# A decoder layer's key projection as a pair of column groups, ahead of the attention projections

## The chip, the cores and the metric

The kernel runs on one core of a Trainium2 chip. The metric is the device time of one execution in microseconds (us), measured three times for the kernel before; lower is better. A profile of one further execution records every instruction with its start and duration, and every DMA packet.

## The reference

One decoder layer, 256 tokens of width 2048, all in float32:

```python
h = rms_norm(x, mix_norm_g)
z = h @ w_in
mq, mk, mv, mo, mi, mf, fq, fk, fv, ff = split(z)
ha = mlstm_chunkwise(mq, mk, mv, ig, lf)          # 4 heads of 256; gates ig, lf from mi, mf
ha = rms_norm(ha) * sigmoid(mo)
hb = forgetting_attention(norm(fq), norm(fk), fv, logf)   # 8 heads of 128; logf from ff
x = x + concat(ha, hb) @ w_out
x = x + (gelu(conv3(a)) * g) @ w_down             # a, g = split(rms_norm(x) @ w_up)
x = x + sigmoid(rms_norm(x) @ w_ple_gate) * (p @ w_ple_proj)
```

`w_in` has 7184 columns: mq, mk, mv, mo with 1024 each, then the gates mi and mf (8), fq, fk, fv (1024 each) and ff (8). Everything that this text is about happens in the product with `w_in` and in the two token mixers that eat its columns.

## The kernel before, in words

**Blocks.** Each large product is a list of blocks, run in order by `run_stream`. A block brings one piece of a weight matrix (128 x 1024 floats, 512 KB, or a bit less) from memory into a raw buffer, splits it into two parts, and feeds TensorE. The split keeps float32 accuracy on a fast matmul type: ScalarE (ACT) casts the piece to `hi` (L300), VectorE (DVE) subtracts to get `lo` (L302), and each product is three matmuls, left-hi by hi, left-hi by lo and left-lo by hi. There are three raw buffers (four more, `more`, while the attention columns are computed), four buffers of parts, and splits are written up to three blocks ahead of the block that is multiplied.

**Two kinds of groups.** A `token_group` computes 512 columns: 8 blocks, each two rows of 128 of the inner dimension, 12 matmuls of 512 columns a block (L356 to L358). A `pair_group` computes two neighbouring pieces of n columns at once: 12 plain blocks ("p") of 12 matmuls with n columns, and two *sevens* ("a" and "b", four blocks each), a Strassen-like scheme that does the work of 24 matmuls with 21, three products for each of seven, at the price of sums of weights on DVE (L440, L441, L451, L452) and of four extra PSUM banks P1, P5, P6, P7. When both sevens are done, `combined` turns these banks into four correction tiles `z_fox` in the tile `spare`, and when the whole group is done, `evac` and `added` bring result and correction together. The order of a pair group is written out as a string, `FOX_ORDER`: four p, then a and p in turn, then b and p in turn, and a last p. Sums of the left side, `S_h`, are made once and used by every pair group. The matmuls of both kinds of groups go through `three` (L367 to L369) or directly through `token_group`.

**Order of the stage.** First 512 columns from mi on (a token group, while x is loaded, normalised and turned); then three pair groups of 430, 430 and 428 columns, which finish the gates, fq, fk and fv (below: the fox groups); then token groups in pairs for mq, mk, mv and mo; then w_out as two pair groups of 512 columns.

**Side work.** The mixers themselves are generators in the deque `side`. After each block `pull(2)` runs two of their steps, taken in turn from the first two generators of the deque, also where a step only finds that it has to wait. `gate_math` computes the gates in seven steps and puts a row for each head into memory (`kept_rows`), from which `row` spreads it to all partitions; `fox_heads` runs the eight attention heads in two generators, six steps a head; `mlstm_scores`, `mlstm_out` and `mlstm_gate` run the mLSTM heads. Ahead of w_out's fifth block `pull_all` runs whatever is left. The framework under this plans each engine's order from its own model of when things are ready, so an engine's rows in the trace don't always stand in the order of the source.

**Turning tiles.** Heads need their queries and keys with features on partitions. `square` transposes 32 x 32 squares on DVE (L204), and `move` then sends 16 DMAs from the POOL (GpSimd) queue (L210) that put the squares in place. `qk_squares(pair)` does that for two attention heads (`qky` to `qkz`, in the tags "sq" and "col"), and its reader waits until seven blocks have passed (`since(7, ...)`). For mq, `qk_group` evacuates into `mz`, squares into `my` (both in `spare`) and moves straight into `mqT`; for mk it moves into a buffer of the tag "zb", and `mk_columns` copies that to `mkT` (L759).

Of the kernel before, what the change touches and what calls it, by code (L numbers as in the profile page):

```python
# [9 lines left out]
F32 = mybir.dt.float32  # L10
# [5 lines left out]
P = 128  # L16
# [15 lines left out]
FOX_ORDER = "pppp" "apapapap" "bpbpbpb" "p"  # L32
GATED = 1032

BLK = 1024
# [26 lines left out]
def layer_kernel(  # L62
# [133 lines left out]
    def squares(name):  # L196

        return mp.tile([P, NT, 4, 128], F32, tag="sq", name=name)
# [308 lines left out]
    with mixers:  # L507
# [72 lines left out]
        def fox_norm(name, off):  # L580
            def gen():
# [12 lines left out]
                for t in range(NT):  # L594
                    v = zz[:, t, off : off + 1024].rearrange("p (h d) -> p h d", h=FH)
                    dve.tensor_mul(v, v, r[:, t * FH : (t + 1) * FH].unsqueeze(2).broadcast_to([P, FH, FD]))
                    yield
            side.append(gen())

        qkz = {}  # L600

        def qk_squares(pair):

            y = squares("qky")
            for c, (zz, off) in enumerate(((z["fq"], 8), (z["fk"], 0))):
                for t in range(NT):
                    square(y, t, 2 * c, zz[:, t, off + pair * 256 : off + (pair + 1) * 256])
            qkz[pair] = gather(y, "qkz")

        g = {}  # L610

        def gate_math():
            def gen():
# [32 lines left out]
                for tt in range(NT):  # L646
                    pe.transpose(bk[:12, tt * P : (tt + 1) * P], aF[:, tt, :], ident)
                aFT = mp.tile([P, 512], F32, tag="qk", name="aFT", bufs=2)[:12, :S]
                dve.tensor_copy(aFT, bk[:12, :S])
                kept_rows("F", aFT)  # L650
                for h in range(2):
                    row("F", 4 + h)
                yield

                M = mp.tile([P, 512], F32, tag="qk", name="M", bufs=2)[:4, :S]
                dve.tensor_tensor_scan(out=M, data0=aFT[0:4, :], data1=aFT[0:4, :], initial=0.0,
# [8 lines left out]
                act.activation(em, m, AF.Exp, scale=-1.0)  # L665
                g.update(Fs=Fs, aF=aF, em=em)
                yield
            side.append(gen())

# [15 lines left out]
        def fox_heads():  # L685
            zv = z["fv"]

            def gen(heads):
                while "em" not in g:
                    yield  # L690
                scale = FD ** -0.5
                for h in heads:
# [7 lines left out]
                    taken.add(h)  # L700
                    if h ^ 1 in taken and h // 2 + 1 < FH // 2:
                        qk_squares(h // 2 + 1)
                    yield
# [41 lines left out]
                    yield  # L745
            qk_squares(0)
            side.append(gen(range(0, FH, 2)))
# [7 lines left out]

        def mk_columns(grp, start):
            while not since(7, start):
                yield
            act.copy(mkT[:, 4 * grp : 4 * grp + 4].rearrange("p k (a j) -> p k a j", j=32),  # L759
                     z["mk"][:, grp].rearrange("p a (k j) -> p k a j", j=32))  # L760
            mk_in.add(grp)
            yield

        def qk_group(name, grp):
            def f(t, b):
                act.activation(mz[:, t], b, AF.Copy, scale=r1["t"][:, t : t + 1])
                square(my, t, 0, mz[:, t])
                if t < NT - 1:
                    return
                if name == "mq":  # L770
                    move(my, mqT[:, grp])
                    return
                if grp == 0:
                    z["mk"] = zbuf("mk").rearrange("p t c -> p (t c)")[:, 0:2048].rearrange("p (g a c) -> p g a c", g=2, c=P)
                move(my, z["mk"][:, grp])
                side.append(mk_columns(grp, done[0]))
            return f
# [166 lines left out]

        z_fox = [spare[:, 2048 + 512 * i : 2560 + 512 * i] for i in range(4)]
        for g_, n in enumerate(FOX_HALVES):

# [19 lines left out]

            def combined(p1, p5, p6, p7, n=n):
                z_ = [v[:, :n] for v in z_fox]
                act.copy(z_[0], p1)  # L970
                dve.tensor_add(z_[1], p6, z_[0])
                dve.tensor_add(z_[2], p7, z_[1])
                for i in (1, 3):
                    dve.tensor_sub(z_[i], p5, z_[i // 2 + 1])

            blocks.extend(pair_group(w_in, lambda: hT, c0, n, FOX_ORDER, ("mm", "aux") if g_ % 2 == 0 else ("aux", "mm"),
                                     S_of, evac_half, added, combined))
            c0 += 2 * n
# [873 lines left out]
```

## Time and profile before

| | |
|---|---|
| median of 3 runs | 1228.82 us (1228.74 to 1228.92) |
| the profiled execution | 1229.07 us |
| its span, first to last instruction | 1227.4 us |
| TensorE (PE) busy | 1219.6 us, 99% |
| weight loads (PEld) busy | 1025.9 us, 84% |
| DVE / ACT / POOL busy | 1023.6 / 761.4 / 179.1 us |
| granted TensorE clock | 0.999 |
| DMA | 276.36 MB, mean 225 GB/s |

The span is the time between the core's first and last instruction; the execution's own time is 1.67 us longer. A matmul's row has the time from its start to the end that is modelled for it, and matmuls overlap: how fast PE works is read from the distance of their starts, not from the durations. The three fox groups run from 32.7 to 141.5 us of the span, mq to mo from there to 341.3 us, w_out to 432 us, and the feed-forward part and the last gate take the rest. Idle time of an engine is put down to what released it; a row of that kind for an engine that isn't the bottleneck costs nothing by itself.

### The profile page before, as it was taken

The page shows a single profiled execution, that of the slowest core. Times are in us where ns is not written, and L with a number is a line of the kernel's source. Part 1 is how long each engine was busy: PE and PEld are TensorE (multiplying, and loading weights), DVE is VectorE, ACT ScalarE, POOL GpSimd, SP SyncE. Part 2 cuts the span into 40 slices and gives each one's busy share as a digit, 9 for nine tenths or more (in the row PEclk, how much of TensorE's full clock was granted, in tenths as well). Part 3 has the DMA queues.
Part 4 walks back from the last instruction along what each step waited for, and adds up shares of the span by engine and source line. Part 5 has one row for each costly group of instructions (what it writes and reads, how often), then busy time and mean ns, then how long its engine had stood idle before and what let it go on. Part 6 is the DMA issues. An engine that isn't in the chain of part 4 may idle for free.

```text
span 1227.4 us, 16369 instructions
## 1 busy us (share of the span) xinstructions
PE 1219.6 (99%) x5547; PEld 1025.9 (84%) x5547; DVE 1023.6 (83%) x1287; ACT 761.4 (62%) x1115; POOL 179.1 (15%) x331
## 2 busy tenths in 40 slices
PE   9999999999999999999999999999999999999998
PEld 7999988888888888888888888888888888888887
DVE  6788857675679989788998898898788999999796
ACT  8567545565655665766676676757657555556653
POOL 2011237243301401011101101110110000050000
PEclk9999999999999999999999999999999999999999
DMA  9566677676565787777687678757796896876552
GB/s 307 181 197 195 175 229 222 183 218 194 164 234 179 234 254 238 241 220 239 202 274 240 188 252 265 229 174 223 236 315 238 293 374 205 268 248 209 193 206 68
DMA packets 126964, 276.36 MB, mean 225 GB/s; under 512 B 14793, under 2 KB 26817, under 8 KB 126881
## 3 DMA queue, kind: packets, MB, share of 16 engines
q1 hardware_dynamic: 115344, 257.27, 65.7%
q0 software_dynamic: 11008, 17.76, 5.2%
q8 instruction: 43, 0.70, 0.2%
q10 hardware_dynamic: 529, 0.30, 0.1%
q14 instruction: 40, 0.33, 0.1%
HBM read 247.99 MB, written 8.93 MB: 209 GB/s over the span
## 4 chain that ended last, share of the span: by engine, by line
PE 99%; DMA 0%; DVE 0%; SPq 0%; ACT 0%; issue 0%; DVEq 0%
PE up L369 12%; PE up L367 12%; PE up L368 12%; PE tg L357 6%; PE tg L356 6%; PE tg L358 6%; PE pg L367 5%; PE pg L368 5%; PE pg L369 5%; PE gt L369 2%; PE gt L368 2%; PE gt L367 2%; PE dnP L1349 1%; PE dnP L1350 1%; PE dnP L1348 1%; PE upP L369 1%
## 5 line engine op out<-in xcount | busy, mean ns | idle before, releaser
L368 PE MATMUL up<-part,x2T 128*128 128x512 f32 x608 | 236.6, 389 | 0.0
L369 PE MATMUL up<-part,x2T 128*128 128x512 f32 x608 | 236.1, 390 | 0.0
L1298 ACT CAST part<-raw 128x1024 fp32r<-128x1024 f32 (+1 forms) x144 | 145.3, 1020 | 104.7 <-PE up L369 36.3
L302 DVE TENSOR_TENSOR lo<-raw,hi 128x1024 fp32r<-128x1024 f32 (+3 forms) x119 | 139.2, 1173 | 76.9 <-ACT hi L300 76.6
L367 PE MATMUL up<-part,x2T 128*128 128x512 f32 x608 | 185.9, 389 | 0.0
L1300 DVE TENSOR_TENSOR part<-raw,part 128x1024 fp32r<-128x1024 f32 (+1 forms) x141 | 165.1, 1179 | 21.1 <-ACT part L1298 15.5
L300 ACT CAST hi<-raw 128x1024 fp32r<-128x1024 f32 (+3 forms) x119 | 120.2, 1012 | 97.4 <-PE tg L358 46.2
L368 PEld LDWEIGHTS up<-part,x2T 128*128 128x128 f32 x608 | 114.1, 188 | 23.7
L367 PEld LDWEIGHTS up<-part,x2T 128*128 128x128 f32 x608 | 114.1, 188 | 23.6
L369 PEld LDWEIGHTS up<-part,x2T 128*128 128x128 f32 x608 | 114.0, 188 | 23.5
L358 PE MATMUL tg<-hi,hT 128*128 128x512 f32 x288 | 113.6, 395 | 0.0
L357 PE MATMUL tg<-lo,hT 128*128 128x512 f32 x288 | 113.3, 393 | 0.0
L356 PE MATMUL tg<-hi,hT 128*128 128x512 f32 x288 | 112.4, 396 | 0.0
L210 POOL DMA_DIRECT2D EZ<-Y x66 | 35.2, 540 | 365.7 <-issue 204.7
L1298 ACT CAST part<-u36r 128x1024 fp32r<-128x1024 f32 (+1 forms) x46 | 47.9, 1044 | 34.6 <-PE up L369 17.2
L1300 DVE TENSOR_TENSOR part<-u36r,part 128x1024 fp32r<-128x1024 f32 (+1 forms) x46 | 55.6, 1209 | 9.4 <-ACT part L1298 5.2
L357 PEld LDWEIGHTS tg<-lo,hT 128*128 128x128 f32 x288 | 54.1, 188 | 11.1 <-DVE lo L302 0.2
L358 PEld LDWEIGHTS tg<-hi,hT 128*128 128x128 f32 x288 | 54.1, 188 | 10.9
L356 PEld LDWEIGHTS tg<-hi,hT 128*128 128x128 f32 x288 | 53.8, 188 | 10.7
L1300 DVE TENSOR_TENSOR part<-u32r,part 128x1024 fp32r<-128x1024 f32 (+1 forms) x44 | 50.3, 1148 | 14.1 <-ACT part L1298 11.6
L1298 ACT CAST part<-u32r 128x1024 fp32r<-128x1024 f32 (+1 forms) x44 | 43.3, 992 | 23.8 <-PE up L369 9.0
L368 PE MATMUL pg<-lo,hT 128*128 128x430 f32 (+1 forms) x156 | 55.7, 357 | 0.0
(924 smaller groups left out, 2770.7 us busy)
## 6 DMA issues: line engine op xcount, KB each, us to landing
raw<-in_w_up_dram SPq DMA_DIRECT2D x78, 512.0 KB, 4.9
raw<-in_w_in_dram SPq DMA_DIRECT2D x71, 512.0 KB, 4.3
u36r<-in_w_up_dram SPq DMA_DIRECT2D x43, 512.0 KB, 5.1
raw<-in_w_down_dram SPq DMA_DIRECT2D x41, 512.0 KB, 5.9
u32r<-in_w_up_dram SPq DMA_DIRECT2D x34, 512.0 KB, 4.9
xs<-in_w_up_dram SPq DMA_DIRECT2D x21, 512.0 KB, 4.9
w2b<-in_w_down_dram SPq DMA_DIRECT2D x20, 512.0 KB, 5.2
raw<-in_w_out_dram SPq DMA_DIRECT2D x17, 512.0 KB, 4.9
```

What stands on the lines that cost most here:

```text
L210: (other if other and (4 * a + b) % 3 else pool).dma_start(out=c[32 * b : 32 * b + 32, a::4], in_=y[32 * a : 32 * a + 32, :, b])
L300: act.copy(hi, raw)
L302: dve.tensor_sub(lo, raw, f32(hi))
L356: pe.matmul(o, ah, hi[:, i, :], start=first, stop=False)
L357: pe.matmul(o, ah, lo[:, i, :], start=False, stop=False)
L358: pe.matmul(o, al, hi[:, i, :], start=False, stop=last)
L367: pe.matmul(o, ah, hi, start=start, stop=False)
L368: pe.matmul(o, ah, lo, start=False, stop=False)
L369: pe.matmul(o, al, hi, start=False, stop=stop)
L1298: act.copy(r32(hi), raw)
L1300: dve.tensor_sub(r32(lo), raw, hi)
L1348: pe.matmul(o, ah, hi, start=first, stop=False)
```

## The change

mk, until now two token groups behind mq, becomes one pair group of twice 512 columns with two sevens, and it stands ahead of the three fox groups. It evacuates into the place of `mqT`, which is empty by then, takes its corrections from `z_fox`, squares into `spare` (the places of `mz` and `my`), and moves to the second half of `spare`, the place of `z_fox`. Its readers `mk_columns` wait for 9 and 12 blocks. The two PSUM tags of the fox groups change places. The queries and keys of the attention heads are squared in other places: pair 0 in `mqT`, as soon as fk is normalised; pair 2 in the second half of `spare`; pairs 1 and 3 as before; and each pair one pair earlier. `gate_math` is no longer in the deque: its seven steps hang behind mq's first five blocks, 2, 2, 1, 1 and 1 of them. The heads start when `Fs` is there, one step ahead of `em`. Two small tiles of the gates move to the tag "WT". `mlstm_scores` is appended behind mq.

```diff
+GATE_STEPS = (2, 2, 1, 1, 1)
...
+                if name == "fk":
+                    qk_squares(0)
...
-            y = squares("qky")
+            if pair % 2:
+                y, c_ = squares("qky"), mp.tile([P, NT * 4, 128], F32, tag="col", name="qkz")
+            else:
+                v = spare[:, 2048:4096] if pair else mqT.rearrange("p g a c -> p (g a c)")
+                y = v[:, 0:1024].rearrange("p (t b c) -> p t b c", t=NT, b=4)
+                c_ = v[:, 1024:2048].rearrange("p (a c) -> p a c", c=P)
...
-            qkz[pair] = gather(y, "qkz")
+            move(y, c_)
+            qkz[pair] = c_, done[0]
...
-                aFT = mp.tile([P, 512], F32, tag="qk", name="aFT", bufs=2)[:12, :S]
+                aFT = mp.tile([P, 384], F32, tag="WT", name="aFT", bufs=4)[:12, :S]
...
+                g.update(Fs=Fs, aF=aF)
                 yield
-                M = mp.tile([P, 512], F32, tag="qk", name="M", bufs=2)[:4, :S]
+                M = mp.tile([P, 384], F32, tag="WT", name="M", bufs=4)[:4, :S]
...
-            side.append(gen())
+            gate_steps.append(gen())
...
-                while "em" not in g:
+                while "Fs" not in g:
...
-                    if h ^ 1 in taken and h // 2 + 1 < FH // 2:
-                        qk_squares(h // 2 + 1)
+                    if h ^ 1 in taken and h // 2 + 2 < FH // 2:
+                        qk_squares(h // 2 + 2)
...
-            qk_squares(0)
+            qk_squares(1)
...
-        def mk_columns(grp, start):
-            while not since(7, start):
+        def mk_columns(grp, zk, start):
+            while not since(9 + 3 * grp, start):
                 yield
             act.copy(mkT[:, 4 * grp : 4 * grp + 4].rearrange("p k (a j) -> p k a j", j=32),
-                     z["mk"][:, grp].rearrange("p a (k j) -> p k a j", j=32))
+                     zk[:, grp].rearrange("p a (k j) -> p k a j", j=32))
...
+        def mk_group():
+            v = mqT.rearrange("p g a c -> p (g a c)").rearrange("p (t c) -> p t c", t=NT)
+            zk = spare[:, 2048:4096].rearrange("p (g a c) -> p g a c", g=2, c=P)
+            def evac(t, h, b):
+                act.activation(v[:, t, h * 512 : (h + 1) * 512], b, AF.Copy, scale=r1["t"][:, t : t + 1])
+            def added():
+                ys = [spare[:, i * BLK : (i + 1) * BLK].rearrange("p (t b c) -> p t b c", t=NT, b=4) for i in range(2)]
+                for h in range(2):
+                    for t in range(NT):
+                        w_ = v[:, t, h * 512 : (h + 1) * 512]
+                        dve.scalar_tensor_tensor(out=w_, in0=z_fox[2 * t + h], scalar=r1["t"][:, t : t + 1],
+                                                 in1=w_, op0=ALU.mult, op1=ALU.add)
+                for h in range(2):
+                    for t in range(NT):
+                        square(ys[h], t, 0, v[:, t, h * 512 : (h + 1) * 512])
+                for h in range(2):
+                    move(ys[h], zk[:, h])
+                    side.append(mk_columns(h, zk, done[0]))
+            return pair_group(w_in, lambda: hT, C_MK, 512, FOX_ORDER, ("mm", "aux"), S_of, evac, added, combined(512))
...
+        blocks.extend(mk_group())
         for g_, n in enumerate(FOX_HALVES):
...
-            blocks.extend(pair_group(w_in, lambda: hT, c0, n, FOX_ORDER, ("mm", "aux") if g_ % 2 == 0 else ("aux", "mm"),
-                                     S_of, evac_half, added, combined))
+            blocks.extend(pair_group(w_in, lambda: hT, c0, n, FOX_ORDER, ("aux", "mm") if g_ % 2 == 0 else ("mm", "aux"),
+                                     S_of, evac_half, added, combined(n)))
...
         for c in range(2):
-            add(C_MQ + c * 512, 512, qk_group("mq", c))
-        for c in range(2):
-            add(C_MK + c * 512, 512, after(qk_group("mk", c), *([mlstm_scores] if c else [])))
+            add(C_MQ + c * 512, 512, after(mq_group(c), *([mlstm_scores] if c else [])))
+        for i, n in enumerate(GATE_STEPS):
+            with_after(blocks[until + i], lambda n=n: [next(gate_steps[0]) for _ in range(n)])
```

More of the change, by code (lines that the diff above doesn't have):

```diff
@@ L607, in qk_squares @@
                     square(y, t, 2 * c, zz[:, t, off + pair * 256 : off + (pair + 1) * 256])
-            qkz[pair] = gather(y, "qkz")
+            move(y, c_)
+            qkz[pair] = c_, done[0]
         g = {}
+        gate_steps = []
         def gate_math():
@@ L665, in gen @@
                 act.activation(em, m, AF.Exp, scale=-1.0)
-                g.update(Fs=Fs, aF=aF, em=em)
+                g["em"] = em
                 yield
-            side.append(gen())
+            gate_steps.append(gen())
         kept, ready = {}, {}
@@ L754, in layer_kernel, with mq_group @@
         mk_in = set()
-        def mk_columns(grp, start):
-            while not since(7, start):
+        def mk_columns(grp, zk, start):
+            while not since(9 + 3 * grp, start):
                 yield
             act.copy(mkT[:, 4 * grp : 4 * grp + 4].rearrange("p k (a j) -> p k a j", j=32),
-                     z["mk"][:, grp].rearrange("p a (k j) -> p k a j", j=32))
+                     zk[:, grp].rearrange("p a (k j) -> p k a j", j=32))
             mk_in.add(grp)
             yield
-        def qk_group(name, grp):
+        def mk_group():
[17 more added lines that the diff above has]
+            return pair_group(w_in, lambda: hT, C_MK, 512, FOX_ORDER, ("mm", "aux"), S_of, evac, added, combined(512))
+        def mq_group(grp):
             def f(t, b):
@@ L767, in f @@
                 square(my, t, 0, mz[:, t])
-                if t < NT - 1:
-                    return
-                if name == "mq":
+                if t == NT - 1:
                     move(my, mqT[:, grp])
[L772 to L776, printed above, removed]
             return f
@@ L945, in layer_kernel, with combined, f @@
         z_fox = [spare[:, 2048 + 512 * i : 2560 + 512 * i] for i in range(4)]
+        def combined(n):
+            def f(p1, p5, p6, p7):
+                z_ = [v[:, :n] for v in z_fox]
+                act.copy(z_[0], p1)
+                dve.tensor_add(z_[1], p6, z_[0])
+                dve.tensor_add(z_[2], p7, z_[1])
+                for i in (1, 3):
+                    dve.tensor_sub(z_[i], p5, z_[i // 2 + 1])
+            return f
+        blocks.extend(mk_group())
         for g_, n in enumerate(FOX_HALVES):
@@ L966, in added @@
                     j()
[L968 to L974, printed above, removed]
-            blocks.extend(pair_group(w_in, lambda: hT, c0, n, FOX_ORDER, ("mm", "aux") if g_ % 2 == 0 else ("aux", "mm"),
-                                     S_of, evac_half, added, combined))
+            blocks.extend(pair_group(w_in, lambda: hT, c0, n, FOX_ORDER, ("aux", "mm") if g_ % 2 == 0 else ("mm", "aux"),
+                                     S_of, evac_half, added, combined(n)))
             c0 += 2 * n
```

## The prediction

> **What bounds the kernel now.** First the busy time by engine and the chain of work that ended last, from the page:
>
> ```profile
> PE 1219.6 (99%) x5547; PEld 1025.9 (84%) x5547; DVE 1023.6 (83%) x1287; ACT 761.4 (62%) x1115; POOL 179.1 (15%) x331
> ...
> PE 99%; DMA 0%; DVE 0%; SPq 0%; ACT 0%; issue 0%; DVEq 0%
> ```
>
> The chain is TensorE from one end to the other. The list of waits of TensorE over the whole span has two rows:
>
> ```profile
> PE xT L172 <- DMA xs<-in_x_dram: 1.5, 1, 1.5
> PE warm L110 <- DVE ones L106: 1.1, 1, 1.1
> ```
>
> Both lie in the first 10 us. The busy time of each stage (columns: stretch, its length, then busy us and count for PE, PEld, DVE, ACT, POOL, clock, DMA share, GB/s) says the same, with DVE at two thirds to four fifths:
>
> ```profile
> 32.70:141.50 108.80, 108.80 (x559) 104.87 (x558) 89.11 (x122) 71.13 (x143) 9.18 (x6) 1.00 0.60 181
> 141.50:341.30 199.80, 199.80 (x924) 166.52 (x923) 129.91 (x233) 110.37 (x182) 85.73 (x160) 1.00 0.72 206
> ...
> 1222.30:1227.40 5.10, 0.01 (x1) 0.00 (x0) 2.32 (x10) 0.70 (x2) 0.00 (x0) 0.86 0.26 85
> ```
>
> "Busy" could still hide slow matmuls, because their rows overlap. So I look at the distance of starts, in the timeline of PE around the seam from mo (a token group) to w_out (a pair group of 512 columns, the form that mk gets):
>
> ```profile
> 338.64 0.39 PE L356 MATMUL tg<-hi,hT 128*128 128x512 f32 x1
> ...
> 341.36 0.39 PE L367 MATMUL pg<-hi,catT 128*128 128x512 f32 x1
> ...
> 344.08 0.84 PE L367 MATMUL pg<-hi,catT 128*128 128x512 f32 x3
> ```
>
> Twelve matmuls lie between each two of these rows: 2.72 us for twelve, 0.2267 us each, in both forms. The time is therefore the number of matmuls times their step, plus 2.6 us at the start and 5.1 us at the end. An edit that lengthens other engines' work costs nothing until it makes TensorE wait, and none can gain more than the matmuls it removes or the waits that remain, and those lie before the change.
>
> **The change, part by part.** *mk as a pair group.* Two token groups are 16 blocks of 12 matmuls, 192. A pair group is 12 plain blocks of 12, 144, and two sevens of 21, 42: together 186. Six matmuls go, 6 x 0.2267 = **1.36 us**. The weights are the same 16 pieces of 512 KB, so the DMA load is the same, 192.5 GB/s at 2.72 us a piece.
>
> The Trainium skill, "TensorE: Matmul & The Clock Gate", section "Back-to-back issue gap", gives about 216 ns for 512 columns as the gap of matmuls alone and 131 ns for a sustained stream of loads and matmuls; by these the six would be 1.30 or 0.79 us. The trace has 227 ns, and the trace decides.
>
> *What the sevens cost elsewhere.* A seven splits 3.5 pieces for two and adds four sums of half a piece. Per pair of pieces that is 3.5 x 1.22 + 4 x 0.69 = 7.0 us on DVE against 21 x 0.2267 = 4.76 us on TensorE; with the plain block that stands between each two of its blocks (four of 1.22 us DVE, 2.72 us PE) the stretch has 11.9 us DVE in 15.6 us. The fox groups run at the same ratio, as all terms go with the number of columns, and let TensorE wait nowhere. So 0, hidden behind the plain blocks; the cover is gone if more than 3.7 us of other DVE work falls into one such stretch.
>
> ```profile
> L302 DVE TENSOR_TENSOR lo<-raw,hi x93: 1009/1224/1228, 29.6 to 343.2; 128x1024 fp32r<-128x1024 f32 x68, 128x860 fp32r<-128x860 f32 x17, 128x856 fp32r<-128x856 f32 x8
> L302 DVE TENSOR_TENSOR lo<-more,hi x35: 593/1049/1057, 32.1 to 136.2; 128x860 fp32r<-128x860 f32 x19, 128x856 fp32r<-128x856 f32 x10, 128x430 fp32r<-128x430 f32 x4, 128x428 fp32r<-128x428 f32 x2
> L1061 DVE TENSOR_TENSOR mqT<-pgP,mqT x2: 687/690/692, 381.5 to 416.4; 128x512 f32<-128x512 f32 x2
> L963 DVE SCALAR_TENSOR_TENSOR fv<-spare,rstd_mix,fv x6: 400/658/662, 108.3 to 146.3; 128x428 f32<-128x428 f32 x4, 128x176 f32<-128x176 f32 x2
> L204 DVE STREAM_TRANSPOSE spare<-spare x8: 670/705/711, 163.8 to 280.2; 128x512 f32<-128x512 f32 x8
> ```
>
> *The seam from mk to the first fox group.* Here DVE has `combined`, 4 x 0.69 = 2.8 us, and then `added`: four corrections, 0.66 x 512/428 = 0.79 us each, and four square transposes of 0.70, 6.0 us. TensorE then holds three split fox blocks of 12 x 0.195 = 2.34 us (step of the 430-column rows: 558 matmuls in 108.8 us), 7.0 us, and needs the fourth's `lo`, 1.05 us. If all of `added` stands before that split, 6.0 + 1.05 = 7.0: just in time. If `combined` is late as well, TensorE waits 2.8 us. Bounds 0 and 2.8; I take 0, because at the same seam of the first two fox groups the planner lets splits pass between the sums:
>
> ```profile
> 66.36 0.60 DVE L971 TENSOR_TENSOR spare<-pgP,spare 128x430 f32<-128x430 f32 x1 [0.72 <-PE pgP L369]
> 66.91 1.05 DVE L302 TENSOR_TENSOR lo<-raw,hi 128x860 fp32r<-128x860 f32 x1
> 67.89 0.60 DVE L972 TENSOR_TENSOR spare<-pgP,spare 128x430 f32<-128x430 f32 x1
> 68.40 1.05 DVE L302 TENSOR_TENSOR lo<-raw,hi 128x860 fp32r<-128x860 f32 x1
> ```
>
> *mk's move and `mkT`.* The same 32 DMAs from POOL and the same two copies on ACT of 1.05 us, but now inside the first fox group. POOL has room: it sat idle for 50 us before the norm of fq, its next work. What is new is the waiter: ACT's copies, behind which ACT's casts for the next blocks are queued.
>
> ```profile
> POOL r_fq L185 <- DVE rs_v L184: 50.2, 1, 50.2
> ...
> L210 POOL DMA_DIRECT2D mk<-spare x32: 536/536/558, 252.0 to 289.5; - x32
> L759 ACT COPY mkT<-mk x2: 1043/1052/1062, 279.0 to 299.3; 128x1024 f32<-128x1024 f32 x2
> ...
> 207.04 8.56 POOL L210 DMA_DIRECT2D qkz<-qky  x16 [4.20 <-ACT qk L698]
> ...
> 251.97 3.78 POOL L210 DMA_DIRECT2D mk<-spare  x7
> ...
> 265.32 0.54 POOL L210 DMA_DIRECT2D mk<-spare  x1 [2.65 <-issue]
> ```
>
> Counted from the seam, the squares of the first half are done at +3 to +5 us. Sixteen issues take 8.6 us (207.04) to 13.9 us (251.97 to 265.86), a landing 3.8 us. All 32 have landed at +24 to +37 us. In the source the second copy is due after the group's 11th block, +20.5 us (p 2.34, first block of a seven 0.59, the others 1.17). Bounds: 0 if the planner puts the copy in ACT's order behind the landing; if ACT is parked at it, the 15th block, due at +25.8, gets copy, cast and subtraction (1.05 + 0.85 + 1.05) after the landing: 1.2 to 14 us late. I take 0: in mk's stage before, the copies ran at 279.0 and 299.3, behind their moves (issued 252 to 266 and up to 290) and 30 to 40 us behind their turn in the source (after the 34th and 38th block of the stage, 3.1 us each: about 248 and 260), and neither that row nor any other ACT row between 33 and 341 us shows a wait for such a move. Deferred, the copy must still free the place of `z_fox` before the fox group's own `combined` at +33.4; at the high end it is 4 us late, and TensorE, which needs those banks for the next group at +36.3, waits up to about 2.4 us.
>
> *Gates and heads behind mq.* No matmul is added or removed: 8 heads, 4 mLSTM heads and the gates issue the same rows. Per run of small matmuls TensorE loses the same whether two heads' runs stand alone or together: here one head and two heads.
>
> ```profile
> 204.50 0.39 PE L357 MATMUL tg<-lo,hT 128*128 128x512 f32 x1
> ...
> 205.61 0.40 PE L356 MATMUL tg<-hi,hT 128*128 128x512 f32 x1
> ...
> 226.06 0.39 PE L356 MATMUL tg<-hi,hT 128*128 128x512 f32 x1
> ...
> 227.82 0.40 PE L358 MATMUL tg<-hi,hT 128*128 128x512 f32 x1
> ```
>
> Less two plain steps, one head's output costs 1.11 - 0.45 = 0.66 us, two together 1.76 - 0.45 = 1.31. So 0. The 48 blocks behind the fox groups (64 before) still hold the side work: gates fill the first blocks, 48 steps of the heads at two a block end at block 27, scores and outputs (16 steps and their waits) at block 37, and the mLSTM gates wait for mo as before; nothing more is left for `pull_all`. The same number of squares, moves and rows is issued. The mk groups' clash over `mz` and `my` goes, but TensorE did not wait for it.
>
> **Sum.** 1229.07 - 1.36 = 1227.71 us for the profiled execution (span 1227.4 - 1.36 = 1226.0); its median companion is 0.25 us lower: **1227.46 us**.
>
> **Rivals.** *A, slower: ACT parked at mk's copies.* Place: the first fox group, 20 to 35 us behind mk. It decides from a landing later than +22.9 us with the copy at its turn in the source. Price 1.2 to 14 us: 1228.7 to 1241.5 us, middle about 1235. For it: the landing is at +24 even at the fast rate. Against: the deferred copies above. [...] Chance 0.10.
>
> *B: the gain is spent at the seams.* DVE's 8.8 us behind mk, or the late place of `z_fox`, cost 1 to 2.8 us: 1228.5 to 1230.2 us. For it: just in time by my sum. Against: planned splits pass. Chance 0.10.
>
> *C, faster by more: TensorE's step falls.* The weight loads take 188 ns of each 227 and are busy 84%. If the blocks were paced by something that the new order removes, mk's 186 matmuls could run at 0.188: 1.36 + 186 x 0.039 = 8.6 us, 1220.2 us.
>
> ```profile
> L358 PEld LDWEIGHTS tg<-hi,hT 128*128 128x128 f32 x288 | 54.1, 188 | 10.9
> ```
>
> Against it: w_out's pair groups, the very form, step at 0.2267. The Trainium skill, "Perfetto Trace Analysis", section "Identifying the Most-Contended Engine", holds that matmul busy time misjudges TensorE and that the weight loads' share should be used; by it 16% would be open, but equal steps of 0.2267 in a stretch without waits say that the share is just 188 over 227. Chance 0.02.
>
> *D: crowded loads behind the fox groups.* With heads and gates earlier, more moves meet the loads while only three raw buffers are left. A load took 6.3 us there:
>
> ```profile
> raw<-in_w_in_dram SPq DMA_DIRECT2D x6, 512.0 KB, 6.3
> ```
>
> (median between 190 and 206 us, DMA 85% busy from 191 to 201). Three buffers give 8.16 us a round, less the split of 2.2 leaves 6.0; at 6.3 a block slips 0.1 us, covered by the three split blocks. At 10 us for a dozen blocks it would slip 16 us, 8 of them covered: 1235 us. Chance 0.03.
>
> **How the numbers follow.** Forecast 0.75, A 0.10, B 0.10, C 0.02, D 0.03. A measurement of this kernel tells about 0.2%, 2.46 us, from no change: below 1226.36 is faster, above 1231.28 slower. Faster: C and a little of the forecast's edge, 0.03. Slower: D, and the four fifths of A that cost over 3.8 us, 0.11. The rest, forecast and B included, is within: 0.86. The range takes the forecast's edge for unseen small terms on the low side (0.7 us) and B whole on the high one: 1226.7 to 1230.3; A's upper part, C and D are left out.
>
> **What would show it.** Right: PE steps of 0.227 in mk's rows (pair-group rows with 512 columns and hT from about 33 us), 186 of them in 42.2 us; no new row in TensorE's waits; span 1226.0. The seam: DVE rows L963 and L204 of mk with L302 among them. The copies L759 near 110 us without idle time ended by a DMA. A would show as idle ACT before L759 or a cast, followed by a PE wait for `lo`; B as a PE wait at the first or second fox group's start; D as casts waiting for raw. Wrong altogether: PE waits elsewhere, or steps that differ from 0.227.

## The result: 0.7% slower, and where the time went

The changed kernel takes **1237.18 us** (median of 6 runs, 1236.26 to 1239.11) against 1228.78 us (1228.62 to 1228.92) of the kernel before on the same chip: a ratio of **1.0069** with a 95% interval of 1.0059 to 1.0079. Predicted were 1227.46 us with a range of 1226.7 to 1230.3, and a chance of 0.11 for slower. The profiled execution took 1236.9 us, its span is 1235.2 us; the span before was 1227.4, so 7.8 us have to be found. Line numbers behind the change are some ten to thirty higher than before: L368 to L370 are the pair groups' matmuls, L357 to L359 the token groups', L301 and L303 the two halves of a split, L211 the moves, L222 and L223 the columns.

The page of the changed kernel, busy time and the chain of work that ended last:

```profile
PE 1224.1 (99%) x5541; PEld 1027.7 (83%) x5541; DVE 1036.7 (84%) x1307; ACT 765.4 (62%) x1122; POOL 177.7 (14%) x331
...
PE 94%; ACT 2%; DVE 2%; DMA 1%; issue 0%; ACTq 0%; DVEq 0%
```

The six matmuls are gone (5541 for 5547), yet PE is busy for 4.5 us more, and the chain, 99% PE before, now runs 5% through other engines. Both say that a stage has changed. Its list of PE's waits:

```profile
PE pg L368 <- ACT catT L222: 3.3, 1, 3.3
...
PE pg L368 <- DVE spare L980: 0.9, 1, 0.9
PE upP L368 <- DVE x2T L165: 0.7, 1, 0.7
```

These three rows are new. The starts of a few matmuls divide the span, here in the timeline of PE, the kernel before and then the one after; rows at the same place of the program:

```profile
141.44 0.35 PE L369 MATMUL pg<-hi,hT 128*128 128x428 f32 x1
...
427.05 0.39 PE L369 MATMUL pg<-hi,catT 128*128 128x512 f32 x1
...
1124.38 0.39 PE L367 MATMUL gt<-part,x3T 128*128 128x512 f32 x1
```

```profile
184.81 0.35 PE L370 MATMUL pg<-hi,hT 128*128 128x428 f32 x1
...
341.02 0.39 PE L368 MATMUL pg<-hi,catT 128*128 128x512 f32 x1
...
433.38 0.39 PE L370 MATMUL pg<-hi,catT 128*128 128x512 f32 x1
...
1132.20 0.39 PE L368 MATMUL gt<-part,x3T 128*128 128x512 f32 x1
```

With the first matmul of a token group (7.45 and 7.00 us) and the start of w_out before (341.36) the stages are:

| stage | before | after | difference |
|---|---|---|---|
| ahead of the first group | 7.45 | 7.00 | -0.45 |
| to the last matmul of the fox groups | 133.99 | 177.81 | +43.82 |
| to the first matmul of w_out | 199.92 | 156.21 | -43.71 |
| to the last matmul of w_out | 85.69 | 92.36 | **+6.67** |
| to the first matmul of the last gate | 697.33 | 698.82 | +1.49 |
| to the end | 103.02 | 103.00 | -0.02 |

The sum is +7.80. The move itself, 43.82 less 43.71, costs 0.11 us in place of gaining 1.36: a wait of 1.03 us at the second fox group, and 0.44 us that I did not trace. Two matmuls of `up` (0.45 us) stand ahead of w_out's last matmul before (383 PE rows in that stage) and behind it after (381), so w_out itself loses 7.1 us and the stage behind it 1.0. Nearly all is lost in w_out, in two ways. First the wait, in the timeline of PE after:

```profile
351.67 0.39 PE L370 MATMUL pg<-hi,catT 128*128 128x512 f32 x1
355.39 0.80 PE L368 MATMUL pg<-hi,catT 128*128 128x512 f32 x1 [3.33 <-ACT catT L222]
355.98 0.63 PE L369 MATMUL pg<-lo,catT 128*128 128x512 f32 x1
356.41 0.63 PE L368 MATMUL pg<-hi,catT 128*128 128x512 f32 x1
```

Between 351.67 and 355.39 lie 3.72 us where the step is 0.227: 3.49 us lost. Then the steps are 0.427 us: the rows follow each other at 355.98 and 356.41. That is the second way, and the windows show its reason in the granted clock (columns: stretch, length, busy us and count of PE, PEld, DVE, ACT, POOL, then the clock):

```profile
341.02:355.30 14.28, 11.04 (x49) 8.82 (x47) 8.72 (x16) 9.38 (x18) 6.28 (x12) 0.98 0.60 194
355.30:361.50 6.20, 6.11 (x18) 4.72 (x19) 6.20 (x13) 1.71 (x5) 0.00 (x0) 0.50 0.43 153
361.50:380.00 18.50, 18.50 (x83) 15.15 (x82) 15.54 (x21) 11.36 (x14) 0.00 (x0) 1.00 0.48 157
```

The clock stood at half from 354.7 to 361.5, 6.8 us. It fell 0.7 us before the wait ended, so 6.1 us of it lie on work, and about half of these, 3.0 us, is lost. That makes 6.5 of the 7.1 us; the rest is not traced.

What PE waited for are the columns 0 to 3 of `catT`, the first two mLSTM heads' output, which POOL moves and ACT casts. POOL and ACT after:

```profile
337.35 4.29 POOL L211 DMA_DIRECT2D haz<-hay  x8 [3.35 <-issue]
343.02 4.22 POOL L211 DMA_DIRECT2D haz<-hay  x8 [1.38 <-DMA haz<-hay]
347.26 1.43 POOL L186 TENSOR_TENSOR rh<-rs_v,neghalf 128x2 f32<-128x2 f32 x2
```

```profile
351.46 1.99 ACT L301 CAST hi<-raw 128x1024 fp32r<-128x1024 f32 x2 [2.66 <-DMA raw<-in_w_out_dram]
...
353.88 1.04 ACT L301 CAST hi<-morex 128x1024 fp32r<-128x1024 f32 x1
354.83 1.70 ACT L222 ACTIVATE catT<-haz,vT 128x256 fp32r<-128x256 f32 x4
```

The moves were issued from 337.4 to 347.2, around the start of w_out at 341.0. These moves took 3.2 to 5.4 us from issue to landing, 4.7 in the median, so the last can have landed by about 351.4; ACT, behind a load and four casts, reaches the columns only at 354.8, and PE wanted them at 351.9. So most of the 3.5 us is ACT's order: the columns stand behind the load's casts. The load itself is not new. In the kernel before, the same load ended ACT's wait 10.7 us behind the start of w_out, after the change 10.4, and PE lost nothing, because the columns stood ahead of it in ACT's order: the moves had gone out 8 us ahead of w_out, and the columns began at 343.1, nine microseconds before PE wanted them (four plain blocks behind 341.36, 10.9 us). Before:

```profile
L210 POOL DMA_DIRECT2D haz<-hay x16: 536/536/596, 323.2 to 332.8; - x16
L221 ACT ACTIVATE catT<-haz,vT x4: 499/502/512, 343.1 to 344.3; 128x256 fp32r<-128x256 f32 x4
```

```profile
352.01 2.01 ACT L300 CAST hi<-raw 128x1024 fp32r<-128x1024 f32 x2 [2.28 <-DMA raw<-in_w_out_dram]
```

The smaller wait, at the seam of the first and second fox group, after; timeline of ACT, PE and DVE:

```profile
115.32 1.03 ACT L771 COPY mkT<-spare 128x1024 f32<-128x1024 f32 x1
...
115.82 0.35 PE L370 MATMUL pg<-hi,hT 128*128 128x430 f32 x1
116.39 0.60 DVE L980 TENSOR_TENSOR spare<-pgP,spare 128x430 f32<-128x430 f32 x1 [1.49 <-ACT mkT L771]
...
117.05 0.46 PE L368 MATMUL pg<-hi,hT 128*128 128x430 f32 x1 [0.87 <-DVE spare L980]
```

The second copy of mk out of the place of `z_fox` runs at 115.3, though POOL had issued its last move by 101.1; DVE may write that place only behind it, and PE gets the banks 1.03 us late (1.23 less a step of 0.20).

### The profile page after: what moved, and what is told of

It is laid out like the page before. It is cut to its first block, busy times and chain, and to the rows that moved or that the text cites. A ratio compares the mean times of both kernels' runs of the same rounds, so it can differ in the third digit from the quotient of the medians.

```text
span 1235.2 us, 16364 instructions
## 1 busy us (share of the span) xinstructions
PE 1224.1 (99%) x5541; PEld 1027.7 (83%) x5541; DVE 1036.7 (84%) x1307; ACT 765.4 (62%) x1122; POOL 177.7 (14%) x331
## 4 chain that ended last, share of the span: by engine, by line
PE 94%; ACT 2%; DVE 2%; DMA 1%; issue 0%; ACTq 0%; DVEq 0%
PE up L370 11%; PE up L368 11%; PE up L369 11%; PE pg L368 5%; PE pg L369 5%; PE pg L370 5%; PE tg L357 4%; PE tg L358 4%; PE tg L359 4%; PE gt L370 2%; PE gt L368 2%; PE gt L369 2%; PE dnP L1382 1%; PE dnP L1381 1%; PE dnP L1380 1%; PE upP L368 1%
## 5 line engine op out<-in xcount | busy, mean ns | idle before, releaser
L370 PE MATMUL up<-part,x2T 128*128 128x512 f32 x608 | 235.6, 389 | 0.0
L303 DVE TENSOR_TENSOR lo<-raw,hi 128x1024 fp32r<-128x1024 f32 (+3 forms) x112 | 130.8, 1170 | 69.4 <-ACT hi L301 68.9
L368 PE MATMUL up<-part,x2T 128*128 128x512 f32 x608 | 185.4, 389 | 0.0
L301 ACT CAST hi<-raw 128x1024 fp32r<-128x1024 f32 (+3 forms) x112 | 112.6, 1008 | 91.8 <-PE pg L370 31.8
L368 PEld LDWEIGHTS up<-part,x2T 128*128 128x128 f32 x608 | 114.1, 188 | 23.6
L370 PEld LDWEIGHTS up<-part,x2T 128*128 128x128 f32 x608 | 114.0, 188 | 23.6
L358 PE MATMUL tg<-lo,hT 128*128 128x512 f32 x224 | 88.5, 395 | 0.0
L359 PE MATMUL tg<-hi,hT 128*128 128x512 f32 x224 | 87.9, 394 | 0.0
L211 POOL DMA_DIRECT2D EZ<-Y x66 | 35.2, 540 | 359.2 <-issue 205.1
L357 PE MATMUL tg<-hi,hT 128*128 128x512 f32 x224 | 86.6, 394 | 0.0
L369 PE MATMUL pg<-lo,hT 128*128 128x430 f32 (+2 forms) x208 | 76.0, 365 | 0.0
L370 PE MATMUL pg<-hi,hT 128*128 128x430 f32 (+2 forms) x208 | 75.7, 365 | 0.0
L1332 DVE TENSOR_TENSOR part<-u32r,part 128x1024 fp32r<-128x1024 f32 (+1 forms) x44 | 50.3, 1146 | 12.5 <-ACT part L1330 10.7
L368 PE MATMUL pg<-hi,hT 128*128 128x430 f32 (+2 forms) x208 | 58.5, 366 | 0.9 <-DVE spare L980 0.9
L303 DVE TENSOR_TENSOR lo<-more,hi 128x860 fp32r<-128x860 f32 (+5 forms) x46 | 45.5, 1007 | 14.8 <-ACT hi L301 14.7
```

What stands on the lines that cost most here:

```text
L211: (other if other and (4 * a + b) % 3 else pool).dma_start(out=c[32 * b : 32 * b + 32, a::4], in_=y[32 * a : 32 * a + 32, :, b])
L301: act.copy(hi, raw)
L303: dve.tensor_sub(lo, raw, f32(hi))
L357: pe.matmul(o, ah, hi[:, i, :], start=first, stop=False)
L358: pe.matmul(o, ah, lo[:, i, :], start=False, stop=False)
L359: pe.matmul(o, al, hi[:, i, :], start=False, stop=last)
```

## The experiments

The theory after the traces, the **late side chain**: gates, heads, scores and outputs form a chain that needs its time; mk's 16 blocks no longer stand between its start (the end of the fox groups) and its customer (w_out), so its end comes too late. Rivals: the **seam** (mk's place collides with the fox groups), and **crowding** (the gates in mq's blocks and the new moves hold the heads up). A third, late loads of w_out, is weakened by the load's rows above: it comes no later than before.

**pe_heads**: heads 0 and 1 go as heads 2 and 3 do, turned by PE.

```diff
-                early = heads[0] == 0
+                early = False
```

> The changed kernel, with the gated outputs of mLSTM heads 0 and 1 turned by TensorE (two runs of four 128x128 transposes, as heads 2 and 3 have it) in place of eight square transposes on DVE, 32 moves and four columns. Late side chain (the mk blocks that stood between the heads and w_out are gone, so those columns come late, TensorE waits 3.3 us for them and then runs at half clock): the wait for catT L222 goes, the granted clock stays at 1.00 through w_out, about 7 us come back less about 1 us for eight more transposes: 1230 to 1231.5 us. Seam theory (the cost is mk's late place at the second fox group, about 115 us): 1236.5 to 1238 us. Crowded gates and heads: they end as late as now and TensorE waits for the transposed heads instead, 1234 to 1238 us.

Measured 1231.66 us, 0.2 above the range, ratio 1.0023 (1.0013 to 1.0032); full clock through w_out. PE's waits and the 16 transposes of the four heads:

```profile
PE pg L368 <- DVE spare L980: 0.9, 1, 0.9
PE upP L368 <- DVE x2T L165: 0.6, 1, 0.6
```

```profile
L909 PE MATMUL hap<-ident,mv x16: 270/272/273, 342.3 to 348.6; 128*128 128x128 f32 x16
```

The wait and the half clock are gone, though ACT still waits 1.4 us for the same load (to 351.1). The w_out wait owns the loss. Without the moves, heads 2 and 3 are early too (at 348.6 done; 361.9 in the changed kernel): their `rh` no longer stands behind the moves in POOL's queue. What keeps this kernel 2.5 us of span behind the kernel before (the stages as above: +0.3, +43.5, -43.7, +1.1, +1.3) is the wait at the seam, the eight transposes more, which I put at 1 us by eight steps of the `hap` kind, and the last stage ahead of the gate, of which below.

**zk_mqT**: mk's squares go to the place of `mqT`.

```diff
-            zk = spare[:, 2048:4096].rearrange("p (g a c) -> p g a c", g=2, c=P)
+            zk = mqT
```

> The changed kernel, with mk's moved squares in mqT's place (2,048 elements, free from mk's squares to the first squares of q and k) in place of the upper half of spare, where the fox groups' z_fox stands. Late side chain: only the wait of about 1.0 us at the end of the first fox group goes, 1236.0 to 1236.4 us, the wait in w_out stays. Seam theory: if the delay there is what shifts all behind it, 1228 to 1230 us.

Measured 1237.05 us, 1.0071 (1.0056 to 1.0086): no difference from the changed kernel, and 0.65 us above the range, which had counted the wait at the seam as gained. The wait at the seam is gone, and the fox groups end 1.1 us sooner behind the first group. But w_out's wait has grown, with the half clock behind it:

```profile
PE hap L909 <- ACT catT L222: 5.9, 1, 5.9
```

What PE gains ahead of w_out the side chain doesn't gain: w_out starts sooner (2.3 us of that are ten of the mLSTM outputs' matmuls, `mob`, which now stand behind its start) and waits longer. The seam is not the cause.

**gates_deque**: the gates' steps as ordinary side work.

```diff
-            gate_steps.append(gen())
+            side.append(gen())
...
-        for i, n in enumerate(GATE_STEPS):
-            with_after(blocks[until + i], lambda n=n: [next(gate_steps[0]) for _ in range(n)])
```

> The changed kernel, with the gates' steps back in the queue of side work in place of mq's first five blocks (the heads still start at Fs, the new places of the squares stay). Late side chain: the cover is as short as in the changed kernel, and the gates come no earlier than before: 1236 to 1241 us, with the wait for catT L222 at least as long. Crowded gates and heads: without the hooks the chain runs as before, 1228 to 1231 us.

Measured 1245.63 us, 1.0140 (1.0124 to 1.0155), above the range given. PE's waits:

```profile
PE hap L909 <- DVE mv L906: 7.4, 1, 7.4
...
PE hap L909 <- ACT junk L877: 2.2, 1, 2.2
```

The hooks behind mq's blocks are worth 8.4 us here; crowding by the hooks is refuted. They don't quicken the gates themselves (the row of gates was turned 25.7 us behind the fox groups here, 25.8 in the changed kernel) but the heads: the last head's output came 151 us behind the fox groups, against 129. Why the heads gain so much is not shown.

**gates_only**: the kernel before with that part of the change alone (hooks, heads waiting for `Fs`, new places of the squares), mk as before.

> The kernel before, with the gates and heads of the change alone (gates' steps behind mq's first five blocks, heads start at Fs, first squares at fk's norm, even pairs of squares in their own places); mk stays two token groups behind mq. Late side chain: 64 blocks of cover stay, the columns are there long before w_out, 1228.3 to 1229.3 us, no new wait. Crowded gates and heads: slower by itself, 1231 us or more, with the heads' end or a wait of TensorE to show it.

Measured 1228.68 us, 1.0002 (0.9992 to 1.0011), no new wait. The gates' edit is free where 64 blocks follow, as the prediction had it.

**late_cols** and **late_cols_mqT**: w_out's first group takes the columns of heads 2 and 3 first, without and with the `zk` of above.

```diff
-OUT_K = (8, 9, 10, 11, 12, 13, 14, 15, 0, 1, 2, 3, 4, 5, 6, 7)
+OUT_K = (8, 9, 10, 11, 12, 13, 14, 15, 4, 5, 6, 7, 0, 1, 2, 3)
```

> The changed kernel, with w_out's first group taking catT's columns 4 to 7 (turned by TensorE) before columns 0 to 3 (the moved ones): the moved columns are wanted four plain blocks and half of the second seven later, some 15 us. Late side chain: the wait for catT L222 goes, and with it the half clock; what may be left is a shorter wait for heads 2 and 3 (hap), below 2 us and without half clock. 1229.5 to 1232 us. If w_out waits for something else that is late (raw loads, the sums S_o), the order changes nothing: 1236 to 1238 us.

> The changed kernel, with both: mk's moved squares in mqT's place, and catT's columns 4 to 7 ahead of 0 to 3 in w_out's first group. Late side chain: no wait at the second fox group (1.0 us less than late_cols) and none at half clock in w_out; what the six matmuls bring can show: 1227.5 to 1230 us, against 1228.7 of the kernel before. If the two halves of the loss are one cause, it is no better than late_cols alone: 1229.5 to 1232 us.

Measured 1240.19 us, 1.0092 (1.0076 to 1.0107), and 1238.11 us, 1.0071 (1.0059 to 1.0084). Both missed what the late side chain was given, and late_cols lies above even the 1236 to 1238 us of "something else that is late": not the moved columns alone are late. The wait of PE in late_cols (in late_cols_mqT `hap` waits 5.4 us), then its DVE:

```profile
PE hap L909 <- DVE mv L906: 6.5, 1, 6.5
```

```profile
351.93 1.23 DVE L303 TENSOR_TENSOR lo<-raw,hi 128x1024 fp32r<-128x1024 f32 x1 [1.82 <-ACT hi L301]
...
357.75 1.67 DVE L906 SCALAR_TENSOR_TENSOR mv<-mv,rh,mo 128x256 f32<-128x256 f32 x4
```

The gating of heads 2 and 3 (L906) stands on DVE behind the split and the weight sums of the second seven, and these behind the load that ACT waited for. So the load has a part in the wait, as the rival had it, though it comes no later than in the kernel before.

**hold_cols**: late_cols_mqT, with the moved columns held back in the side work until heads 2 and 3 are turned.

```diff
-                    side.append(columns(gather(y, "haz"), lambda: catT, 0, g_ml))
+                    side.append(behind(columns(gather(y, "haz"), lambda: catT, 0, g_ml)))
+                else:
+                    ha["turned"] = True
...
+        def behind(cols):
+            while "turned" not in ha:
+                yield
+            yield from cols
```

> The kernel late_cols_mqT, with the moved columns 0 to 3 held in the queue of side work until heads 2 and 3 are turned, so that on DVE their subtractions stand behind the gating of heads 2 and 3. Late side chain, and what the run late_cols showed (the order of w_out's blocks brings nothing while DVE's own order keeps heads 2 and 3 behind the late columns): hap runs near 350 us, the columns at 354 are wanted only at about 368, no wait above 1 us in w_out and full clock: 1228 to 1230 us. If the wait has another owner (sums S_o, raw loads of w_out): above 1233 us.

Measured 1238.03 us, 1.0076 (1.0063 to 1.0089), in the range of "another owner"; `hap` waits 6.3 us. The edit did not change what it aimed at: L906 stood ahead of the columns' subtractions on DVE already in late_cols (357.75 and 359.33), and does so here (356.18 and 357.76). POOL and DVE of this kernel:

```profile
347.90 2.11 POOL L211 DMA_DIRECT2D haz<-hay  x4 [0.25 <-DMA haz<-hay]
350.02 2.81 POOL L186 TENSOR_TENSOR rh<-rs_v,neghalf 128x2 f32<-128x2 f32 x2
```

```profile
355.57 0.69 DVE L477 TENSOR_TENSOR S_o<-So_f,S_o 128x512 fp32r<-128x512 f32 x1 [0.69 <-ACT S_o L476]
356.18 1.67 DVE L906 SCALAR_TENSOR_TENSOR mv<-mv,rh,mo 128x256 f32<-128x256 f32 x4
```

The norm of heads 2 and 3 (`rh`, L186) stands behind the 16 moves on POOL, and L906 then behind splits and sums on DVE, one of them waiting for `S_o`. These three edits of the customers' order helped nothing; that none could, because the tail of the chain is late on ACT, POOL and DVE at once, is my reading and not shown.

**mk_tokens_ahead**: mk at its new place, but as the two token groups of before, squares in `my`, moves into the same `zk`.

```diff
-        blocks.extend(mk_group())
+        for c in range(2):
+            add(C_MK + c * 512, 512, mk_tokens(c))
```

> The changed kernel, with mk at its new place ahead of the fox groups but as the two token groups of the kernel before (no sevens, six matmuls more). It tells the move from the form. Late side chain (the move costs, the form does not): w_out waits as in the changed kernel, and its half clock follows, while the wait at the second fox group may go, since mk's moves start earlier and half by half: 1235.5 to 1239 us. If the form (sevens, its burst on DVE) is what costs: 1228.5 to 1231 us.

Measured 1238.20 us, 1.0075 (1.0061 to 1.0088), with the wait in w_out and none at the seam:

```profile
PE hap L909 <- ACT catT L222: 6.5, 1, 6.5
```

So the **move** costs, not the form. One small thing goes with the form: from w_out's last matmul to the last gate this kernel takes 697.38 us, as before, and every kernel with the pair group 0.9 to 1.7 us more; in each of them PE waits for `x2T` at the first `up` groups (0.2 to 0.9 us). The two matmuls of `up` that stand inside w_out before and in this kernel, and behind it in the others, are 0.45 us of it; why `x2T` is late is open.

**cover**: the changed kernel with 196 matmuls more in mv's blocks, with a zero matrix on the left.

```diff
+                if bi and len(starts) == 8 and C_MV <= c0 < C_MO:
+                    for i in range(14):
+                        pe.matmul(st["b"][i % 2][:, :n], Zr, hi[:, 0, :], start=False, stop=False)
```

> The changed kernel, with 196 matmuls of a zero 128x128 against the block's own hi (512 columns) added to mv's two groups, 14 in each block behind the first of a group: 44.4 us of TensorE that load nothing and change nothing, in place of the 43.5 us that mk's blocks took out from between the heads and w_out. Cover theory (the side chain needs its time, whatever the blocks compute): the wait for catT L222 and the half clock go, 44.4 - 3.5 - 3.4 = 37.5 us, 1274 to 1276 us. If the chain is late for another reason (its order, its queues, DMA): the waits stay, 1280 to 1283 us.

Measured 1276.13 us. The 44.4 us of added work cost 38.95 us: 5.5 are given back (6.3 by the stages from w_out's start on). From the fox groups to w_out are 201.78 us now, and from w_out's start to the last gate 784.9 in place of 791.2, full clock. PE's waits, then the moves and ACT's columns:

```profile
PE upP L374 <- DVE x2T L165: 0.9, 1, 0.9
PE pg L374 <- DVE spare L986: 0.9, 1, 0.9
```

```profile
L211 POOL DMA_DIRECT2D haz<-hay x16: 533/534/596, 371.7 to 382.1; - x16
L222 ACT ACTIVATE catT<-haz,vT x4: 498/500/503, 389.3 to 390.5; 128x256 fp32r<-128x256 f32 x4
```

The moves go out 5 us ahead of w_out (387.5) again, and ACT's columns begin 1.7 us behind its start, as before the change. The added matmuls load nothing and feed nothing; they give back time, and the wait and the half clock vanish. By itself this would fit anything that lacks time ahead of w_out, the loads too; with the load's rows (no later than before) and pe_heads (no moves, no wait) it decides for the late side chain. The total is 0.1 us above the range, since the added rows took 45.57 us of the stage, not 44.4.

**pulls3**: three steps of side work behind each block for two.

```diff
-        run_stream(blocks, 2, more, ramp=True)
+        run_stream(blocks, 3, more, ramp=True)
```

> The changed kernel, with three steps of side work taken behind each block in place of two. It tests the count that the prediction used (steps per block) as what sets the end of heads and outputs. If steps per block set it, the heads end a third earlier in the order, the moves of haz go out well before w_out and the wait and the half clock go: 1229.5 to 1231.5 us. If the chain is set by its own latencies and its places in the queues (each head waits for moves, rows and the head before it), the heads end within some 10 us of where they do now and w_out still waits: 1234 to 1240 us.

Measured 1241.41 us, 1.0096 (1.0079 to 1.0113), 1.4 above the range of the second case; w_out waits 8.5 us, at `hap`. The matmuls of the heads' outputs, as groups with the first and last start, in the kernel before, the changed one and this one:

```profile
L741 PE MATMUL ob<-PT,fv x16: 377/378/382, 204.7 to 283.9; 128*128 128x256 f32 x16
```

```profile
L753 PE MATMUL ob<-PT,fv x16: 377/378/382, 260.0 to 314.1; 128*128 128x256 f32 x16
```

```profile
L753 PE MATMUL ob<-PT,fv x16: 377/378/382, 259.0 to 313.6; 128*128 128x256 f32 x16
```

Behind the end of the fox groups the last one comes at 142.5, 129.3 and 129.3 us. Half as many steps again per block change nothing: the steps that the source takes per block don't set the heads' end here. What does set it was not isolated.

**pe_heads_mqT**: both repairs at once.

> The kernel pe_heads, with mk's moved squares in mqT's place as in zk_mqT. Both losses gone at once. If they add up: pe_heads less 1.0 us, 1230.3 to 1231.0 us, no wait of TensorE but the one at the first up group (0.2 to 0.7 us). If removing the seam only moves the wait elsewhere, as it did in zk_mqT: 1231.5 us or more.

Measured 1231.71 us, 1.0020 (1.0010 to 1.0029), not told apart from pe_heads, and in the range given for a wait that moves elsewhere. The list has no new wait in w_out, though. The wait at the seam is gone; the profile has 0.9 us of waits for x at the start that the changed kernel's did not have, so one profile can't say whether the 1.0 us would show.

**stalls**: the kernel before with a chain PE, POOL, PE in each of the eight token groups, to measure the clock.

```diff
+        for b in banks:
+            pe.matmul(b[:16, 0:16], Zs, Ts, start=False, stop=False)
+        pool.tensor_tensor(out=Ts[:, :w], in0=ones[:, :w], in1=neghalf[:, :w], op=ALU.pow)
+        for b in banks:
+            pe.matmul(b[:16, 0:16], Zs, Ts, start=False, stop=False)
```

> The kernel before, with one wait made in the middle of each of the eight token groups of mq, mk, mv and mo: two matmuls of 16 columns, a POOL power of 2, 4, ... 16 columns into their right side (0.75 us for 2 and 3.73 us for 16 by the rows of before), and the two matmuls again. It measures which length of wait halves the granted clock. If any wait above some 3 us brings half clock for 6.8 us: none of the first six (up to 2.9 us) does, the last one or two (3.3 and 3.7 us and the signals around them) do, each about 3.4 us beyond itself. If the half clock came from something else in w_out: none does. Sum of the waits about 18 us and 0 to 7 us of half clock: 1246 to 1256 us.

One run, 1281.96 us: the expected sizes missed, since PE's order put other work into some of these chains, and the waits came out other than built. They serve all the same. Timeline and windows around three of them:

```profile
190.62 0.63 PE L748 MATMUL pt<-ident,L 128*128 128x128 f32 x3 [2.50 <-DVE L L744]
...
222.09 0.75 PE L748 MATMUL pt<-ident,L 128*128 128x128 f32 x3 [3.25 <-DVE L L744]
...
347.85 0.27 PE L346 MATMUL tg<-Ts,Zs 128*16 128x16 f32 x4 [2.79 <-POOL Ts L344]
```

```profile
191.70:195.10 3.40, 3.40 (x16) 2.78 (x15) 0.43 (x1) 1.11 (x4) 3.40 (x8) 0.50 0.27 67
...
222.40:225.80 3.40, 3.33 (x12) 2.58 (x12) 0.88 (x4) 1.33 (x3) 3.07 (x6) 0.50 0.51 161
...
348.70:352.10 3.40, 3.40 (x10) 2.65 (x9) 0.00 (x0) 0.00 (x0) 0.00 (x0) 0.50 0.55 173
```

Waits of 2.50, 2.79 and 3.25 us each brought 3.41 us of half clock, not the 6.8 expected of a wait above 3 us; the longest, 8.3 us, brought 10.24.

## Why the prediction was wrong, step by step

*What bounds the kernel*: right as read, steps of 0.227 and no waits. But a profile without waits says nothing of how near the next one is, and I did not measure the slack of the one customer of the side chain.

*mk as a pair group, -1.36 us*: 186 for 192 matmuls, as counted. The net of the two stages around it is 0.11 us, with 1.03 of the wait at the seam and 0.44 untraced in it.

*The sevens, 0*: right; no wait of PE in mk's rows.

*The seam from mk to the first fox group, 0 of 0 to 2.8*: right; the new wait is one group later.

*mk's move and `mkT`, 0*: missed by a little. The copy was deferred without parking ACT, as taken, but it came too late for the place of `z_fox`: the bound of "up to about 2.4 us" had the right waiter, and it measured 1.03. The reason given there, a slow landing, was not it: the moves were issued by 101.1, and the copy ran at 115.3 by ACT's order.

*Gates and heads behind mq, 0*: **this step failed.** "The 48 blocks behind the fox groups still hold the side work" came from counting source steps, two a block: heads at block 27, scores and outputs at block 37. It took the time of the chain behind the blocks, and with it the cover that leaves with mk, at nothing. pulls3 shows that the count is not what sets the end. The trace of before already contradicted it: the last head's output at 283.9 us is 142.5 us behind the fox groups, the 46th of 64 blocks of 3.12 us, where the count says 27. The last of the four norms behind the outputs ran at 333.3, 8 us ahead of w_out. With 156.2 us to w_out in place of 199.9, and 10.9 us more to the block that wants the columns, 167.1 us are left. After, the heads' outputs end at 129.3, the last move is issued at 161.9, its landing takes 4.7 and the first column 0.5: 167.1 us, without a queue in between. That is already the limit, and ACT's load and casts added the rest of the 3.5 us; the half clock then added 3.0. The sentence "nothing more is left for `pull_all`" fell with it: the gating of heads 2 and 3 and the columns ran inside w_out.

*Rivals.* A, ACT parked: no; the copies' rows show no DMA wait. B: happened in kind, a late place of `z_fox`, within its price of 1 to 2.8 us, but it decides nothing (zk_mqT). C: no; the step stayed at 0.227. D: loads are not late behind the fox groups; one load of w_out took 5.7 us and held ACT for 2.66 us in the worst place, a part of the wait, but it came as early as before the change. The rival that came true, the shortened cover, was not on the list: I counted the blocks that are left, and left out the time that the chain needs. The sign that the prediction gave for "wrong altogether", PE waits elsewhere, is what the trace shows.

*The half clock* was on no list either, and it nearly doubled the loss in w_out. The Trainium skill, "TensorE: Matmul & The Clock Gate", section "HAM oscillation — how this bites in real kernels", warns of idle gaps over about 3.4 us; the measurements here agree with that in kind, but halve the clock for waits from 2.50 us on (last section). By the waits of 3.0 to 3.3 us in these traces, a rival with such a wait would have had to be priced at 4.7 to 6.5 us, the wait and half of the 3.4 or 6.1 us of half clock behind it.

## What to carry to other kernels

When work that lies between a side chain's start and its customer is moved away, compare its latency in the trace of before (the last result's time behind the chain's start) with the time at which the customer wants it, not the number of steps that the order allows. Here the columns began 9 us before they were wanted, and 43.5 us of cover went. This tells that a zero is not safe, and not what the loss will be: the chain itself became shorter (the last move was issued 191.4 us behind the fox groups before, 161.9 after), and so 3.5 us of waiting came of it, not 34. A wait that the profile puts on one late tile may have several behind it: reordering the customers brought nothing three times, while giving time back, or taking the moves out, removed the wait and the half clock. In these traces a wait of TensorE of 2.5 to 3.3 us cost itself and 1.7 to 3.0 us of half clock.

## What the runs showed of the hardware

The granted clock falls to half around a long wait of TensorE, and stays there for 3.41, 6.83 or 10.24 us: multiples of one length. It falls at times on a grid of that length. In `stalls` it fell at 157.57, 191.70, 222.42, 253.14, 287.28, 348.72 and 376.02 us, and these lie 10, 9, 9, 10, 18 and 8 times 3.413 us apart. So the span can be cut into windows of 3.413 us that end at these times. The table has the idle time of each wait, all idle time (from the modelled end of a matmul to the next start) in the window that ends where the clock falls (or, where it doesn't, in the wait's idlest window), and the half clock: its whole length, and the part behind the wait's end, in which work runs slowly.

| kernel, wait | PE idle | idle in the window | half clock | behind the wait |
|---|---|---|---|---|
| changed kernel, second fox group | 0.87 us | 0.87 us | none | none |
| gates_deque, two waits 0.7 us apart, ahead of `hap` | 2.15 and 7.4 | 1.88 (no fall), then 2.67 | 10.24 us | 5.0 us |
| stalls, ahead of `pt` | 2.50 | 2.58 | 3.41 | 3.41 |
| stalls, ahead of the last POOL product but one | 2.79 | 2.55 | 3.41 | 3.41 |
| stalls, ahead of `Fp` | 3.01 | 2.25 | 3.41 | 3.41 |
| stalls, ahead of a later `pt` | 3.25 | 3.08 | 3.41 | 3.41 |
| changed kernel, w_out | 3.33 | 2.63 | 6.83 | 6.1 |
| zk_mqT, w_out | 5.9 | 3.06 | 6.83 | 4.0 |
| pulls3, w_out | 8.5 | 3.41 | 10.24 | 5.9 |

A wait's own length does not settle the price; where it lies among the windows does. In all traces of this case (the first 10 us and the last few left out), a window at full clock with up to 1.88 us idle was followed by full clock, and one with 2.25 us or more by half. Once at half, a window with 0.70 us idle or more was followed by half, and one with 0.15 or less by full. The wait of 3.33 us ran 0.70 us over the end of a window and cost two windows; the one of 3.25 us ended 0.3 us before such an end and cost one. Where between 1.88 and 2.25 us the limit lies, and how far the small matmuls around some of these waits count as work, no run here shows.

The Trainium skill, "TensorE: Matmul & The Clock Gate", section "What's actually happening", says that the clock is set by free-running windows of 3413 ns, half after an idle one and full after a busy one. The lengths and the grid agree with it. That a window has to be idle as a whole does not fit the windows above that were idle for 2.25 to 2.67 us only. While the clock was at half, a 512-column matmul stepped at 0.427 us in place of 0.227.
